# A two-layer encoder trunk: the whole output projection of layer 0 moves into the list schedule, in three rounds, with the residual kept in SBUF

## The chip, the cores and the metric

The kernel runs on one core of a Trainium2 chip. The metric is the device time of one execution in microseconds (us). The kernel before took 1623.58 us in the median of three runs (1622.95 to 1627.89).

## The reference

The input is one sequence of 512 tokens with 1024 channels. Layer 0 mixes with a bidirectional RWKV-7 half (8 heads of 64) and a bidirectional Hyena half (512 channels, long filters through an FFT); layer 1 mixes with 2-D neighbourhood attention. Behind each mixer stand a gated convolutional FFN (width 2816) and a gated per-layer embedding, each added to the residual. The part that the change touches is this one:

```python
z = rmsnorm(h, mix_norm[j]) @ mix_w_in[j]
y_a = rwkv7_bidir(z[..., :RWKV_COLS], ...)          # channels 0 to 511
y_b = hyena_bidir(z[..., RWKV_COLS:], ...)          # channels 512 to 1023
h = h + jnp.concatenate([y_a, y_b], axis=-1) @ mix_w_out[j]
h = h + conv_ffn(h, ...)
h = h + per_layer_embedding(h, p[i], ...)
```

All products of large matrices are computed in float32 to nearly full precision.

## The kernel before

Activations lie channel-major: eight tiles of 128 channels by 512 tokens. A product with a weight is made of three matmuls in the fp32r type: each operand is split into a high part (a copy that rounds, on ScalarE) and a low part (the difference, on VectorE or GpSimd), and high x high, high x low and low x high are added in PSUM. One such matmul streams 512 columns through a 128 x 128 weight tile.

**Two ways of ordering.** Everything behind layer 0's mixer is written in the order in which it runs, by `gemm`: it loads a block of weights into `wraw` (L627), splits it into `whi` (ACT, L613) and `wlo` (DVE, L605) and issues the matmuls into the PSUM tiles `g` (L599). Layer 0's mixer is different. There `nc` is replaced by a recorder, class `Plan`: every call becomes a step with a cost and with the steps it depends on, and `schedule()` then sets the order of all steps on all five engines by a list schedule. Among the steps that can start soonest on an engine (within `AHEAD`) it takes the one with the highest rank: the longest chain of costs behind the step plus 1000 times a number per group from the table `ORDER`. `write()` issues the steps in that order (L562, so nearly all instructions of the mixer carry this line), and each engine keeps it. `nc.gates` holds a group back until some other step is planned. Of the tiles' names, `w` is a tile of the pool of slabs (44 of 128 x 520 values), `wr` a loaded weight tile (3 buffers), `wp` a split part (12 buffers), `b` a PSUM bank (8), `x` and `uv` what a scan loads and updates.

**The groups of the mixer.** `start` loads the input x (eight tiles `w<-in_xT`) and the constants, splits x into `xh`, `xl` and computes the RMS norm: `norm0` squares each tile on ACT and sums over channels with 32 one-column matmuls against a vector of ones (`b<-con,w`). `low` and `z` are the input projection of the RWKV half, `prep` its decays and keys, `inverse` a triangular inverse per head pair (through the DRAM tensors `nd` and `xd`), `scan` the state update over 8 chunks of 64 tokens, `out` its norm and gate, which gives `ys[0]` to `ys[3]`. `hyena` is the input projection of the other half; `filters`, `fparts`, `kf`, `signals`, `ab` and `back` are its convolution by Fourier tables (`dft_f`, `dft_i`), which gives `ys[4]` to `ys[7]`. `emb` computes the p projections of both layers ahead of time and stores them in DRAM (`pj_d`). `early` (`out_early`) multiplies `ys[0]` to `ys[2]` with their rows of the output weight, adds the input x, which it loads a second time, and stores the sum in the DRAM tensors `h_d`.

**Behind the mixer** `outproj0` (L1589) loads `h_d` back into the eight residual tiles `h` and runs the other five of eight rows of the output projection (`LATE`, 4 to 7 and 3) as ordinary `gemm`s: 2 groups of 4 output tiles x 5 rows x 3 = 120 matmuls. The FFN follows. Its `norm` scales the eight tiles into `xh`, `xl`, squares them on ACT into `nsq` (2 buffers) and adds the squares on GpSimd into `nacc`; the sums over channels are needed only at the evictions.

## Time and profile before

| what | us |
|---|---|
| median of three runs | 1623.58 |
| the profiled execution | 1624.16 |
| its span (first to last instruction) | 1622.4 |
| busy TensorE (PE) in it | 1544.8 |
| busy VectorE (DVE) | 978.7 |
| busy ScalarE (ACT) | 719.5 |
| busy GpSimd (POOL) | 325.4 |

About 1.8 us of the profiled execution lie outside its span. PE, DVE, ACT and POOL are engines that work side by side; SP only issues DMAs, in order. A row of the timeline gives the start in us from the span's start, the duration, the engine, the line, the operation, the tiles (out<-in) and the count of merged instructions; in brackets stands the idle time of the engine before it and what ended it. Matmuls overlap, so a row of several tells the pace by its start and the next row's start. fp32 matmuls appear as two records each in the trace and as one in the order.

### The profile page before, as it was taken

Reading aid. Unit: us, or ns where it says so; the run is one execution under the profiler, and the core shown is the slowest. Engines: PE = TensorE matmul, PEld = TensorE weight load, DVE = VectorE, ACT = ScalarE, POOL = GpSimd, SP = SyncE. Lnnn points to the kernel's source line nnn. Section 1 sums busy time; section 2 is a strip of 40 time slices with the busy share of each in tenths; the row PEclk is TensorE's granted clock in tenths of the full one; section 3 lists DMA queues with packets and bytes.
Section 4 is the critical chain, followed back from the end, with each engine's and each line's share of the span. In section 5 each row is a group of like instructions: output and inputs, shape, how many; then the busy total and the mean of one; then the engine's idle time right before and its main releaser. Section 6 shows DMA issues by size and latency. Waiting matters only on the chain.

```text
span 1622.4 us, 24675 instructions
## 1 busy us (share of the span) xinstructions
PE 1544.8 (95%) x9576; PEld 1227.8 (76%) x9576; DVE 978.7 (60%) x1609; ACT 719.5 (44%) x1206; POOL 325.4 (20%) x286
## 2 busy tenths in 40 slices
PE   8999999996886999999999999999999999999998
PEld 6767777764565888888888878778778888888886
DVE  2587585865553766624774664565675665366654
ACT  4553635663432544413443563655554443144332
POOL 3574445533240300000001322011030000000020
PEclk9999999997987999999999999999999999999999
DMA  6366456677454233232324232323112322222421
GB/s 215 96 190 181 133 154 177 214 220 215 145 179 141 100 100 104 91 101 95 95 100 144 90 130 91 111 81 126 61 65 92 104 93 102 91 87 95 166 94 65
DMA packets 116310, 200.16 MB, mean 123 GB/s; under 512 B 27729, under 2 KB 57297, under 8 KB 116194
## 3 DMA queue, kind: packets, MB, share of 16 engines
q1 hardware_dynamic: 116194, 198.59, 38.3%
q8 instruction: 75, 1.23, 0.3%
q14 instruction: 41, 0.34, 0.1%
HBM read 166.04 MB, written 30.93 MB: 121 GB/s over the span
## 4 chain that ended last, share of the span: by engine, by line
PE 85%; DMA 4%; DVE 4%; ACT 2%; SPq 2%; POOL 1%; issue 1%; DVEq 0%; POOLq 0%; ACTq 0%
PE g L599 62%; PE b L562 19%; DVE w L562 3%; SPq L562 2%; PE m L599 1%; PE s L599 1%; DMA wr<-in_dft_f 1%; PE m L1835 1%; POOL w L562 1%; DMA wr<-in_dft_i 1%; ACT w L562 1%; ACT oh L613 0%; DMA pj_d<-w 0%; DMA wr<-in_mix_w_in 0%; DVE ol L605 0%
## 5 line engine op out<-in xcount | busy, mean ns | idle before, releaser
L605 DVE TENSOR_TENSOR wlo<-wraw,whi 128x1024 fp32r<-128x1024 f32 x186 | 235.5, 1268 | 325.8 <-ACT whi L613 321.0
L613 ACT CAST whi<-wraw 128x1024 fp32r<-128x1024 f32 x186 | 193.5, 1041 | 424.4 <-PE g L599 408.1
L599 PE MATMUL g<-xh,whi 128*128 128x512 f32 x872 | 342.0, 392 | 13.2 <-ACT whi L613 13.2
L599 PE MATMUL g<-xh,wlo 128*128 128x512 f32 x872 | 340.6, 391 | 0.0
L599 PE MATMUL g<-xl,whi 128*128 128x512 f32 x872 | 340.3, 390 | 0.0
L599 PEld LDWEIGHTS g<-xh,whi 128*128 128x128 f32 x872 | 164.4, 188 | 48.5 <-ACT whi L613 13.4
L599 PEld LDWEIGHTS g<-xh,wlo 128*128 128x128 f32 x872 | 164.2, 188 | 35.3 <-DVE wlo L605 0.8
L599 PEld LDWEIGHTS g<-xl,whi 128*128 128x128 f32 x872 | 164.3, 188 | 33.9
L605 POOL TENSOR_TENSOR nacc<-nsq 128x512 f32<-128x512 f32 x5 | 9.2, 1833 | 777.3 <-PE g L599 639.7
L562 PE MATMUL b<-xh,wp 128*128 128x512 f32 x416 | 142.2, 416 | 9.1 <-ACT wp L562 9.1
L599 PE MATMUL g<-hh,whi 128*128 128x512 f32 x352 | 137.2, 390 | 0.0
L599 PE MATMUL g<-hh,wlo 128*128 128x512 f32 x352 | 137.0, 389 | 0.0
L599 PE MATMUL g<-hl,whi 128*128 128x512 f32 x352 | 137.0, 389 | 0.0
L602 DVE SCALAR_TENSOR_TENSOR c<-u,prm,c 128x511 f32<-128x511 f32 x176 | 126.5, 747 | 6.4 <-ACT c L608 5.9
L562 PEld LDWEIGHTS b<-xh,wp 128*128 128x128 f32 x416 | 77.8, 192 | 32.6 <-ACT wp L562 10.5
L608 ACT ACTIVATE c<-u,prm 128x512 f32<-128x512 f32 x88 | 70.3, 816 | 70.8 <-DVE u L605 70.8
L562 POOL TENSOR_TENSOR wp<-wr,wp 128x512 fp32r<-128x512 f32 x60 | 80.1, 1350 | 64.9 <-ACT wp L562 30.2
L562 PE MATMUL b<-w 64*64 64x128 f32 (+5 forms) x1692 | 84.3, 253 | 7.3 <-POOL w L562 3.5
L562 POOL TENSOR_TENSOR w<-w 128x256 f32<-128x256 f32 (+2 forms) x72 | 76.6, 1083 | 68.0 <-ACT w L562 41.4
L562 PE MATMUL b<-xl,wp 128*128 128x512 f32 x208 | 85.2, 417 | 0.0
L562 PEld LDWEIGHTS b<-w 64*64 64x64 f32 (+4 forms) x1692 | 62.9, 136 | 26.5 <-issue 9.2
L605 DVE TENSOR_TENSOR u<-g,rstd 128x512 f32<-128x512 f32 x104 | 71.4, 687 | 16.5 <-PE g L599 15.6
(170 smaller groups left out, 2563.4 us busy)
## 6 DMA issues: line engine op xcount, KB each, us to landing
wraw<-in_up SPq DMA_DIRECT2D x88, 512.0 KB, 3.4
wraw<-in_down SPq DMA_DIRECT2D x44, 512.0 KB, 3.5
wr<-in_mix_w_in SPq DMA_DIRECT2D x52, 256.0 KB, 2.9
wraw<-in_na_w_qkv SPq DMA_DIRECT2D x24, 512.0 KB, 3.5
x<-ch_d SPq DMA_DIRECT2D x16, 640.0 KB, 7.2
ch_d<-w SPq DMA_DIRECT2D x64, 128.0 KB, 2.0
wraw<-in_gate SPq DMA_DIRECT2D x16, 512.0 KB, 3.5
tab<-in_rpb SPq DMA_DIRECT2D x8, 768.0 KB, 4.2
```

The lines of the kernel that those rows point to most:

```text
L562: getattr(e, method)(*args, **kw)
L599: return self.nc.tensor.matmul(out, lhsT, rhs, start=start, stop=stop, skip_group_check=not group)
L602: return self.nc.vector.scalar_tensor_tensor(out=out, in0=in0, scalar=scalar, in1=in1, op0=op0, op1=op1)
L605: return (eng or self.nc.vector).tensor_tensor(out=out, in0=in0, in1=in1, op=op)
L608: return self.nc.scalar.activation(out=out, in_=in_, func=func, **kw)
L613: self.nc.scalar.copy(h, src)
L1835: nc.tensor.transpose(pst[:, i], sc[:, i // 2, (i % 2) * P:(i % 2 + 1) * P], ident)
```

## The change

The output projection is now wholly part of the list schedule, in three rounds that add into the residual tiles `h`: `early` (`ys[0]` to `ys[2]`, plus x), `mid` (`ys[4]` to `ys[7]`) and `last` (`ys[3]`), each for two groups of four output tiles. `outproj0` and the DRAM tensors `h_d` are gone. The tiles `h` are allocated before the mixer; x is loaded into them, and until `early` they also serve as scratch for `wa_up`, the low-rank tiles, `rstd0` and the filters' spectra. The pool of slabs shrinks from 44 to 39 and the scan's `x` from 4 buffers to 3. The sum of squares is added up on VectorE, so that 4 one-column matmuls are left of 32. The planner's rules change too: a change of a matmul's shape costs 0.17 in its account, a shape is kept for 1.5 us where another step of it is ready, groups named in `loose` need not wait for their own first step, and the numbers of `ORDER` are new, with a table `MOVED` of exceptions.

```diff
-    HOP, OWN, AHEAD = 0.2, 0.1, 0.2
-    DRAG, SMALL = 0.0, 5
+    HOP, OWN, AHEAD = 0.2, 0.1, 0.15
+    DRAG, SMALL = 0.0, 3
+
+    SWITCH, RUN = 0.17, 1.5
...
-                t, s = max((x for x in c if x[0] <= m), key=lambda x: x[1].rank)
+                c = [x for x in c if x[0] <= m]
+                if e == "tensor" and run < self.RUN:
+                    c = [x for x in c if x[1].form == form] or c
+                t, s = max(c, key=lambda x: x[1].rank)
...
+            ph = self.pool(top, "ph", side="right")
+            self.h = [ph.tile([P, S], F32, name=f"h{k}") for k in range(KT)]
             self.mixer0()
...
-                self.outproj0()
...
-            self.rstd0 = pk.tile([P, S], F32, name="rstd0")
+            self.rstd0 = self.h[4]
...
-            self.sl = self.pool(st, "sl", bufs=self.SLABS, side="right")
             self.wr = self.pool(st, "wr", bufs=3, side="right")
             self.wp = self.pool(st, "wp", bufs=self.PARTS, side="right")
+            self.sl = self.pool(st, "sl", bufs=self.SLABS, side="right")
...
-    SLABS, PARTS = 44, 12
-
-    ORDER = dict(start=200, low=190, filters=77, scan=100, inverse=90, prep=80, z=79, out=60, hyena=50,
-                 fparts=56, kf=39, signals=62, ab=44, back=59, early=30, emb=10)
+    SLABS, PARTS = 39, 12
+
+    ORDER = dict(start=180, x=200, low=198.5, norm=120, filters=75, scan=100, inverse=84, prep=80, z=79, out=60,
+                 hyena=50, fparts=40, kf=67, signals=70, ab=58, back=46, early=30, emb=25, consts=86, mid=72,
+                 last=99)
...
-        xin = [self.slab() for _ in range(KT)]
+        xin = self.h
         for k in range(KT):
+            nc.group = "x", k
             nc.sync.dma_start(out=xin[k], in_=a["xT"][k])
...
+        late = [self.weights("mix_w_out_b", g) for g in range(2)]
+        for g in range(2):
+            nc.gates["mid", g] = self.ys[7][:1]
+            self.part(("mid", g), self.out_late, g, LATE[:4], sources=late[g][:4])
+        for g in range(2):
+            nc.gates["last", g] = [self.ys[LATE[4]][0], ("mid", g)]
+            self.part(("last", g), self.out_late, g, LATE[4:], sources=late[g][4:])
...
+            if acc is None:
+                acc = sq
+            else:
+                self.tt(acc, acc, sq, ALU.add)
+        ps = self.bank(4)
+        for t in range(4):
+            self.mm(ps[:, t:t + 1], acc[:, t * P:(t + 1) * P], self.cst("one"))
...
-            x = xs[q] = rb.tile([P, 2, 5, 2, 64], F32, name="x", bufs=4)
+            x = xs[q] = rb.tile([P, 2, 5, 2, 64], F32, name="x", bufs=3)
...
-            self.tt(xin[j], ps, xin[j], ALU.add)
-            self.put(self.h_d[g * 4 + j], xin[j])
+            self.tt(self.h[g * 4 + j], ps, xin[j], ALU.add)
+
+    def out_late(self, g, ks):
+
+        w = [self.item(len(ks) > 1) for _ in ks]
+        for j in range(4):
+            ps = self.bank()
+            c = slice(j * P, (j + 1) * P)
+            for i, k in enumerate(ks):
+                self.mm3(ps, w[i][0][:, c], w[i][1][:, c], *self.ys[k], i == 0, k == ks[-1])
+            t = self.h[g * 4 + j]
+            self.tt(t, ps, t, ALU.add)
```

**The first loads.** On SP, the first rows of the program; `wr<-in_mix_w_in` are the weight tiles of the input projection. Before:

```order
L724 DMA prm<-in_params 128x126
L562 DMA w<-in_xT 128x512
L562 DMA wr<-in_mix_w_in 128x512 x3
L562 DMA w<-in_feats 17x512
L562 DMA w<-in_xT 128x512 x3
L562 DMA con<-in_const 128x387
L562 DMA w<-in_xT 128x512 x4
L562 DMA prm<-in_params 128x394
L562 DMA w<-in_wa_up 128x512 x2
L562 DMA rcon<-in_rconst 128x1088
L562 DMA gup<-in_g_up 128x512
L562 DMA wr<-in_mix_w_in 128x512 x3
```

And now, behind the first parameters, three tiles of x (`h_73` to `h_75`) and two weight tiles:

```order
L582 DMA h_76<-in_xT 128x512
L582 DMA wr<-in_mix_w_in 128x512
L582 DMA h_77<-in_xT 128x512
L582 DMA h_78<-in_xT 128x512
L582 DMA h_79<-in_xT 128x512
L582 DMA h_80<-in_xT 128x512
L582 DMA con<-in_const 128x387
L582 DMA rcon<-in_rconst 128x1088
L582 DMA gup<-in_g_up 128x512
L582 DMA h_73<-in_wa_up 128x512
L582 DMA prm<-in_params 128x394
L582 DMA wr<-in_mix_w_in 128x512
```

All of x now stands ahead of every constant, and the fourth weight tile behind five loads of constants and parameters.

**The end of the mixer on TensorE.** Before, the inverse transform (`b<-w`, 96 matmuls of 256 columns) ran last, and the out-projection's 120 matmuls into `g` followed:

```order
L562 MATMUL b<-xl_672,w 128x512
L562 MATMUL b<-xh_671,w 128x512 x4
L562 MATMUL b<-w 128x256 x96
L599 MATMUL g<-xh_1150,whi 128x512
L599 MATMUL g<-xl_1151,whi 128x512
```

Now the inverse transform is followed by `early` of one group, the 96 matmuls of `mid`, the 24 of `last` (`xh_811`, `xl_812` are `ys[3]`) and the 48 of layer 1's `emb` (`b<-w,wp`), of which 38 stand in one row just ahead of these; the next `g` belongs to the FFN:

```order
L582 MATMUL b<-xh_811,wp 128x512 x3
L582 MATMUL b<-w,wp 128x512 x2
L582 MATMUL b<-xh_811,wp 128x512
L582 MATMUL b<-xl_812,wp 128x512
L582 MATMUL b<-xh_811,wp 128x512
L582 MATMUL b<-w,wp 128x512 x8
L619 MATMUL g<-xh_6042,whi 128x512
L619 MATMUL g<-xl_6043,whi 128x512
```

No product of the mixer stands behind the eight `emb` matmuls.

**The way into the FFN on ScalarE.** Before, the casts of the out-projection's weights came first and the FFN's scaled tiles and squares were mixed among them:

```order
L562 CAST xh_1162<-w 128x512
L613 CAST whi<-wraw 128x1024 x2
L613 CAST whi<-wraw 128x512
L613 CAST whi<-wraw 128x1024 x2
L608 ACTIVATE xh_6067<-h_5873,prm 128x512
L608 ACTIVATE nsq<-h_5873 128x512
L613 CAST whi<-wraw 128x512
L608 ACTIVATE xh_6071<-h_5874,prm 128x512
```

Now (`COPY w<-b` evicts `emb`'s products, which SP then stores in `pj_d` ahead of the FFN's first weight load):

```order
L582 COPY w<-b 128x512 x4
L628 ACTIVATE xh_6062<-h_78,prm 128x512
L628 ACTIVATE xh_6066<-h_79,prm 128x512
L628 ACTIVATE xh_6070<-h_80,prm 128x512
L628 ACTIVATE nsq<-h_73 128x512
L628 ACTIVATE nsq<-h_74 128x512
L628 ACTIVATE nsq<-h_75 128x512
L628 ACTIVATE nsq<-h_76 128x512
L628 ACTIVATE nsq<-h_77 128x512
L633 CAST whi<-wraw 128x1024
```

The FFN's first weight cast now stands behind three scaled tiles and five squares, with no matmuls of the mixer left beside it.

More of the change, by code (lines that the diff above doesn't have):

```diff
@@ L291, in note @@
             first = self.firsts.setdefault(self.group, s)
-            if first is not s:
+            if first is not s and self.group not in self.loose:
                 s.after[first.n] = True
@@ L339, in price @@
                 t = max(n / 600, 0.223)
+            form = tuple(32 if x <= 32 else 64 if x <= 64 else P for x in (rows, cols))
+            if s.form is None:
+                s.form = form
+            elif form != s.last:
+                t += self.SWITCH
+            s.last = form
             s.cost += t
@@ L447, in start @@
             return t
[L449 removed]
+        lifted, form, run = False, None, 0.0
         while True:
@@ L480, in schedule @@
                     c *= 2
+                if s.form != form:
+                    run = 0.0
+                    c += self.SWITCH
+                form, run = s.last, (run if s.form == s.last else 0.0) + s.cost
             if s.table and s.table != table:
@@ L484, in schedule @@
                 taken[e].append((t, t + c))
-            free[e] = end = t + c
+            s.issue, free[e] = t, t + c
+            end = t + c
             if s.bytes:
@@ L511, in schedule @@
                 x.left -= 1
-                x.at = max(x.at, end + (self.HOP if x.engine != e or s.bytes else self.OWN))
+                x.at = max(x.at, end + (self.HOP if x.engine != e or s.bytes else 0.0 if e == "tensor" else self.OWN))
                 if not x.left:
```

77 lines of the change are left out of this document (37 added, 40 removed).

## The prediction

> **What bounds the kernel now.** I first read the page's shares and slices, then the busy time of each engine by stage, cut where the program changes its work, and then the chain of waits and the timeline at the places where TensorE (PE) stands still.
>
> ```profile
> PE 1544.8 (95%) x9576; PEld 1227.8 (76%) x9576; DVE 978.7 (60%) x1609; ACT 719.5 (44%) x1206; POOL 325.4 (20%) x286
> 0.00:24.40 24.40, 17.04 (x70) 15.27 (x71) 7.29 (x13) 13.96 (x23) 5.86 (x19) 1.00 0.89 300
> 24.40:362.50 338.10, 329.11 (x3395) 244.25 (x3395) 234.67 (x440) 179.69 (x378) 177.84 (x170) 0.98 0.56 166
> 362.50:495.10 132.60, 101.18 (x976) 75.19 (x976) 72.42 (x135) 47.01 (x110) 46.81 (x41) 0.85 0.56 174
> 495.10:508.30 13.20, 0.04 (x1) 0.04 (x1) 4.83 (x9) 2.26 (x3) 0.00 (x0) 0.70 0.65 217
> 508.30:538.60 30.30, 30.26 (x121) 24.31 (x122) 16.68 (x17) 11.74 (x17) 4.82 (x3) 0.91 0.35 114
> 538.60:1622.40 1083.80, 1067.21 (x5017) 868.71 (x5015) 642.83 (x999) 464.86 (x679) 90.06 (x53) 0.99 0.30 99
> ```
>
> Columns of a stage: its length, then busy time of PE, weight loads, DVE, ACT and POOL, the granted clock, the DMA share and GB/s. PE bounds the program, 95% busy, so time can come only from its idle stretches, its slow clock, or its work. The last row, the FFN and all behind it, is 1083.8 us that the change does not touch. The change acts on the 538.6 us ahead: the start, the dense middle (97% busy), the end of the mixer (PE idle for 132.6 - 101.18 = 31.4 us, clock 0.85), a hole of 13.2 us, and the out-projection's 120 matmuls in 30.3 us.
>
> ```profile
> 381.52 2.93 PE L562 MATMUL b<-w,wp 128*128 128x512 f32 x6 [13.53 <-ACT wp L562]
> 412.98 1.22 PE L562 MATMUL b<-w,wp 128*128 128x512 f32 x2 [4.99 <-ACT wp L562]
> 501.35 5.79 DMA wraw<-in_mix_w_out_b
> 508.26 0.79 PE L599 MATMUL g<-xh,whi 128*128 128x512 f32 x1 [13.18 <-ACT whi L613]
> ```
>
> Two timeline rows, one of the chain, one more of the timeline: 18.5 of the 31.4 us are two waits for Fourier tables, and the hole is the wait for the out-projection's first weight, whose load could start only when the mixer's tiles were free.
>
> **The start (term A).**
>
> ```profile
> 5.25 0.72 ACT L562 ACTIVATE xh<-w,prm 128x512 fp32r<-128x512 f32 x1
> prm<-in_params SPq DMA_DIRECT2D x1, 63.0 KB, 1.9
> 6.00 0.75 DVE L562 SCALAR_TENSOR_TENSOR xl<-w,prm,xh 128x512 fp32r<-128x512 f32 x1 [2.88 <-ACT xh L562]
> 10.76 13.81 PE L562 MATMUL b<-con,w 128*128 128x1 f32 x64 [0.31 <-DMA con<-in_const]
> 18.27 0.62 ACT L562 CAST wp<-wr 128x512 fp32r<-128x512 f32 x1 [1.36 <-DMA wr<-in_mix_w_in]
> 0.00:24.40 24.40, 3.40 (x6) 1.66 (x7) 3.49 (x6) 5.01 (x4) 1.00 0.89 300
> ```
>
> The row of `prm` is from the page's list of DMA issues, with its time from issue to landing. The last row is the first stage cut to instructions on `wp` (PE, weight loads, ACT, POOL): by 24.4 us PE had run six matmuls of the input projection and 64 records of the norm, which held it from 10.76 on while the squares arrived one by one. Now only 8 such records remain, later. Ahead of the eighth tile of x stand 63 KB of parameters, 7 more tiles and 3 weight tiles, 2.88 MB with itself; at the window's 300 GB/s that is 9.6 us, and with 1.9 us for the first landing and 0.72 + 0.75 for the split, all of x is ready near 13.5 us and PE has done its 36 first matmuls at 14.5. The fourth weight tile lies 1.70 MB further on, 5.7 us: with landing and cast (0.62) near 18.5 us. From there to 24.4 PE runs 25 more at the 0.235 us found below: 61 instead of 6, 55 x 0.235 = 12.9 us, less 0.9 for the 8 records still to come. **A = 12 us.** Bounds: 7 if the five constant loads delay the fourth weight by 5 us more than their bytes; 16 if loads never hold PE back after 14.5. The seven additions of squares on DVE (7 x 0.61) run beside PE.
>
> **Fewer changes of shape (term B).**
>
> ```profile
> 346.54 0.70 PE L562 MATMUL b<-w,wp 128*128 128x512 f32 x2
> 347.17 0.45 PE L562 MATMUL b<-x,uv 128*64 128x64 f32 x8
> 348.17 1.64 PE L562 MATMUL b<-w,wp 128*128 128x512 f32 x6
> 349.74 0.45 PE L562 MATMUL b<-x,uv 64*64 64x64 f32 x8
> ```
>
> From its start to that of the next row, a run of two takes 0.63 us and one of six 1.57: each matmul 0.235, and 0.16 for the change to another shape. Counted over PE's rows of the two orders, the mixer changes shape 275 times before and 220 now. 55 x 0.16 = 8.8 is the upper bound; where PE waits anyway it is worth nothing. **B = 5 us**, since most changes lie in the dense middle.
>
> **The end of the mixer (term C).** The 120 out-projection matmuls cost the same inside the list, 120 x 0.235 = 28.2 us, and so stay in the sum. What can be gained is the 31.4 us of idle time and the slow clock: at most 0.15 x 101 = 15 us of busy time lost, of which I count 9, because the mean of 0.85 contains the idle stretches. That is 40 us. For cover there are now `emb`'s 96 matmuls (22.6 us), which the order moves from the middle to this stage, and `mid` behind the inverse transform. What is late next, from the order's distances and these rows:
>
> ```profile
> w<-kt_d SPq DMA_DIRECT2D x16, 128.0 KB, 7.0
> w<-in_xT SPq DMA_DIRECT2D x16, 256.0 KB, 4.6
> wr<-in_dft_i SPq DMA_DIRECT2D x8, 256.0 KB, 5.2
> 133.77 2.72 DMA xd<-w
> 145.41 64.74 PE b L562 x839
> L562 DVE TENSOR_TENSOR w<-w 128x512 f32<-128x512 f32 (+16 forms) x120 | 70.5, 609 | 9.8 <-DMA w<-nd 7.2 <-DMA w<-hw_d 0.6
> L562 POOL TENSOR_TENSOR w<-w 128x512 fp32r<-128x512 f32 x16 | 20.6, 1301 | 19.9 <-ACT w L562 19.8
> ```
>
> The last inverse's round trip through `xd` took 133.77 to 145.41 = 11.6 us in head pair 0; the order leaves some 8 us of matmuls beside it: 4 us of wait. Scan 3 needs the `kt_d` loads, 7.0 us, with ten matmuls (2.3) beside them: 5. The spectra put 26 additions and products on DVE (26 x 0.61 = 16 us) and 13 on POOL (17 us) beside the last scan, whose own DVE steps queue behind them, with 21 us of PE work there: 4. `dft_i` is loaded behind four other tiles, 5.2 us and a cast, with 4 us of matmuls left: 3. The second `early` has its weights behind four reloads of x (4.6 us): 3. Together 19 us, and 4 for the clock behind them: 23 stay, **C = 40 - 23 = 17 us**; bounds 0 and 40.
>
> **The way into the FFN (term D).**
>
> ```profile
> 509.50:513.90 4.40, 4.38 (x10) 3.47 (x11) 1.83 (x2) 0.52 (x1) 0.00 (x0) 0.50 0.70 235
> 528.52 1.16 ACT L608 ACTIVATE nsq<-h 128x512 f32<-128x512 f32 x2 [1.08 <-POOL nacc L605]
> L562 ACT COPY w<-b 128x512 f32<-128x512 f32 (+2 forms) x96 | 43.8, 477 | 41.5 <-PE b L562 40.8
> L608 ACT ACTIVATE xh<-h,prm 128x512 fp32r<-128x512 f32 x40 | 32.2, 818 | 13.8 <-DVE h L605 13.8
> L608 ACT ACTIVATE nsq<-h 128x512 f32<-128x512 f32 x40 | 28.2, 721 | 6.0 <-POOL nacc L605 5.7 <-DVE h L605 0.2
> L605 POOL TENSOR_TENSOR nacc<-nacc,nsq 128x512 f32<-128x512 f32 x30 | 49.8, 1659 | 74.4 <-ACT nsq L608 73.1
> L613 ACT CAST whi<-wraw 128x1024 fp32r<-128x1024 f32 x186 | 193.5, 1041 | 424.4 <-PE g L599 408.1 <-DMA wraw<-in_mix_w_out_b 8.2 <-issue 7.8
> wraw<-in_up SPq DMA_DIRECT2D x88, 512.0 KB, 3.4
> ```
>
> The hole does not go; it moves behind the last `emb` matmul. From there ACT has about two of four copies left (1.0), three scaled tiles (2.5), two squares (1.4); then the squares wait for POOL, as they did at 528.52, because `nsq` has two buffers: an addition (1.7), a square (0.7), an addition (1.7), a square (0.7), and only then the cast (1.0): 10.7, say 11 us. The first weight, issued behind the last store of `pj_d` (four copies 1.9, and the issues), would land after 2.5 + 3.4 and be cast at 7; that bounds it from below, and 5.1 us, as this load's sibling needed, does not exceed 11. So 13.2 becomes 11 and both are followed by the same half clock (ten matmuls in 4.4 us where 19 fit, 2.1 us lost): **D = 2 us**; bounds 5 (a hole of 8) and -2.
> The page "TensorE: Matmul & The Clock Gate" of the Trainium skill, section "Architectural detail: the array is 16× 32×32, not 1× 128×128", says that ScalarE and VectorE take their instructions strictly first in, first out. By this rule the cast must wait behind the squares and D stays at 2; if a ready cast could overtake them, D would be 5 and the sum 3 us more. The 1.08 us of ACT idle time at 528.52, with other work queued behind, agree with the rule.
>
> **At no cost.** The `h_d` stores and loads (16 of 256 KB) go; their time is inside the hole. `h` as scratch and 5 slabs fewer free about as much as they take. With 3 buffers a load of the scan's `x` starts once the pair of chunks three places earlier is done, so two pairs of chunks cover it; what it costs without that cover is the last rival.
>
> **Sum.** A 12 + B 5 + C 17 + D 2 = 36 us. The profiled execution took 1624.2 us (1622.4 and 1.8 around it), 0.6 above the median of the runs: 1624.2 - 36 = 1588 us, and 1588 to the nearest microsecond against the median too.
>
> **The rivals.**
>
> *Nearly every wait at the end is covered* (20%). `emb`, `mid` and `last` are 216 matmuls, 51 us of work that needs little else, and a list schedule puts them where PE has nothing else. Then only 5 of the 40 us stay: 12 + 5 + 35 + 2 = 54, 1570 us. Against it: in the order most of `mid` stands behind the last inverse transform, so it cannot cover what lies ahead.
>
> *The end keeps its waits; the three rounds do not do what they say* (18%). `mid` depends on `ys[4]` to `ys[7]`, which come last; if loads through SP's one queue and the in-order DVE and POOL set the pace, the same 31.4 us stay, in other places. C = 0: 12 + 5 + 2 = 19, 1605 us.
>
> *No change that can be measured* (4%): A and B are eaten by the middle, which loses `emb` as cover (24.4 to 362.5 has only 9 us of idle time now) and gains 30.
>
> *Slower: the scan runs out of `x`* (8%).
>
> ```profile
> x<-ch_d SPq DMA_DIRECT2D x16, 640.0 KB, 7.2
> 361.41 0.40 PE L562 MATMUL b<-uv,w 128*64 128x64 f32 x8
> 365.24 0.45 PE L562 MATMUL b<-uv,w 128*64 128x64 f32 x8 [0.52 <-ACT uv L562]
> ```
>
> Two loads of each of the four scans can no longer run ahead into the scan before. If SP holds each until its buffer is free and issues it with nothing in between, 8 x 7.2 = 58 us are exposed: 1588 + 58 = 1646 us. It decides from the point where a load is issued less than 7.2 us ahead of its chunk. Against it: a chunk took 365.24 - 361.41 = 3.8 us with PE nearly free, and two pairs of chunks, 15 us, lie between.
>
> **How the numbers follow.** My forecast has 50%. About 0.3%, 5 us, can be told from no change. The forecast and the first two rivals, 88%, are faster; 4% the same; 8% slower. The bounds of the terms give 7 + 0 + 0 - 2 = 5 us and 16 + 9 + 40 + 5 = 70 us, 1619 and 1554. For 8 of 10 I take 1560 to 1612 us, which holds the first two rivals and leaves the far ends out.
>
> **What would show it.** A: the norm's 64 records shrunk to 8, and PE dense from 18 to 20 us on. B: fewer, longer runs of one shape in the timeline. C: the two waits of 13.5 and 5 us gone, PE idle for about 20 us in the last third of the mixer, and waits for `kt_d`, `dft_i` and DVE in place of `dft_f`. D: a hole of some 11 us ahead of the first `g`, ended by ACT's `whi`, with squares that wait for POOL just before. The forecast is wrong if the middle falls below 97% busy, if the hole is closed, or if scan matmuls wait for `x`.

## The result

The changed kernel takes 1599.7 us in the median of four runs (1595.4 to 1603.9), the kernel before 1625.7 in the same job: ratio 0.984, 95% interval 0.981 to 0.987. A second measurement of the changed kernel gave 1600.8 us and 0.983 (0.981 to 0.985). It is faster, by 26 us between the medians and 25.0 between the spans of the two profiled executions (1622.4 and 1597.4), where 36 were forecast, and lies inside the range of 1560 to 1612. Two runs far above all others, 1923.4 us of the kernel before and 5203.6 us of the version with the new norm alone, are left out of medians and ratios.

The page of the profile after, its span and the shares of the engines:

```profile
span 1597.4 us, 24570 instructions
PE 1527.6 (96%) x9520; PEld 1217.7 (76%) x9520; DVE 975.3 (61%) x1618; ACT 718.5 (45%) x1210; POOL 341.6 (21%) x296
```

The stages of the kernel before, cut at 300 us (columns as in the prediction: length, busy time of PE, weight loads, DVE, ACT, POOL, granted clock, DMA share, GB/s):

```profile
24.40:300.00 275.60, 269.47 (x2545) 200.03 (x2546) 188.53 (x355) 137.15 (x280) 151.20 (x144) 0.99 0.51 149
300.00:495.10 195.10, 160.81 (x1827) 119.40 (x1826) 118.55 (x220) 89.55 (x206) 73.45 (x68) 0.88 0.63 196
```

And of the kernel after: start, middle, end of the mixer, hole, first matmuls of the FFN, the rest:

```profile
0.00:24.40 24.40, 15.49 (x58) 11.77 (x59) 15.60 (x20) 14.60 (x24) 10.26 (x22) 1.00 0.89 292
24.40:300.00 275.60, 265.45 (x2856) 198.66 (x2854) 197.02 (x390) 146.00 (x306) 143.97 (x144) 0.97 0.56 159
300.00:499.40 199.40, 175.15 (x1593) 135.87 (x1592) 121.05 (x213) 87.99 (x196) 92.34 (x76) 0.91 0.55 173
499.40:508.30 8.90, 0.05 (x1) 0.05 (x1) 2.60 (x5) 6.62 (x12) 4.07 (x4) 0.69 0.82 295
508.30:516.60 8.30, 7.33 (x17) 5.30 (x18) 5.43 (x3) 3.56 (x5) 7.42 (x4) 0.51 0.53 147
516.60:1597.40 1080.80, 1064.14 (x5001) 866.04 (x4999) 633.59 (x990) 459.70 (x670) 83.52 (x49) 0.99 0.30 99
```

The mixer of before ended at 495.1 us and left 28.2 us of out-projection to do; now everything is done at 499.4. The middle became worse, 10.2 us of idle time in place of 6.1 and a clock of 0.97 in place of 0.99; the end of the mixer became better, 24.3 us of idle time (199.40 - 175.15) in place of 34.3 (195.10 - 160.81). The hole is 8.9 us in place of 13.2, but 17 matmuls behind it take 8.3 us at a clock of 0.51, 4.0 at their full pace.

**One table for all versions.** The order differs between versions, so a window does not hold the same work. I therefore counted: each matmul of an order at its pace at full clock (0.229 us for 512 columns of fp32r, the others from stretches of the trace in which PE ran dense), summed in the order and laid over the trace. *Lag* is the time minus the work issued by then. The 28 extra one-column matmuls of the old norm, 6.2 us, and 12.3 us of added ones in one experiment count as lag, since they produce nothing.

| version | lag at 50 us | at 300 us | at the mixer's end | its growth from 300 us on |
|---|---|---|---|---|
| before | 25.1 | 39.3 | 94.6 | 55.3 |
| after | 11.0 | 29.0 | 71.4 | 42.4 |
| after, second measurement | 9.8 | 33.3 | 75.9 | 42.6 |
| norm's 32 matmuls back, ahead | 23.5 | 28.9 | 83.8 | 54.9 |
| before, with the new norm alone | 16.0 | 46.6 | 94.3 | 47.7 |
| delay in the same order | 32.8 | 48.9 | 90.5 | 41.6 |
| old numbers | 10.5 | 28.2 | 81.3 | 53.1 |
| emb early again | 11.0 | 30.4 | 93.5 | 63.1 |
| last two rounds outside | 10.5 | 30.6 | 72.9 | 42.3 |
| no keeping, no price of shape | 10.7 | 47.2 | 113.9 | 66.7 |
| price of shape, no keeping | 10.6 | 53.6 | 113.7 | 60.1 |
| squares added on DVE | 10.8 | 30.6 | 74.9 | 44.3 |
| last stores on POOL | 10.3 | 24.7 | 68.2 | 43.5 |
| both: rounds outside, stores on POOL | 10.1 | 26.5 | 66.9 | 40.4 |

Between before and after the lag falls by 14.1 us at the start, rises by 3.8 in the middle (14.2 to 18.0), falls by 12.9 at the end: 23.2. The hole gives 4.3 more. From the FFN's first matmul to the end the kernel takes 1597.4 - 508.25 = 1089.15 us, 5.35 more than the 1083.8 behind the old out-projection; the old half clock had cost 2.1, so 3.3 are lost there. Together 24.2 of the 25.0 us; the rest is the paces in the count. (In the second profile of the changed kernel the middle loses 9.3 in place of 3.8, and the clock behind the hole 0.3 in place of 3.3.)

### The profile page after: what moved, and what is told of

It reads as the page before. It is cut to its first block, busy times and chain, and to the rows that moved or that the text cites. A ratio compares the mean times of both kernels' runs of the same rounds, so it can differ in the third digit from the quotient of the medians.

```text
span 1597.4 us, 24570 instructions
## 1 busy us (share of the span) xinstructions
PE 1527.6 (96%) x9520; PEld 1217.7 (76%) x9520; DVE 975.3 (61%) x1618; ACT 718.5 (45%) x1210; POOL 341.6 (21%) x296
## 4 chain that ended last, share of the span: by engine, by line
PE 82%; DVE 6%; DMA 4%; ACT 3%; SPq 2%; issue 1%; POOL 1%; POOLq 0%; DVEq 0%; ACTq 0%
PE g L619 61%; PE b L582 17%; DVE w L582 4%; SPq L582 2%; PE m L619 2%; PE s L619 1%; DMA wr<-in_mix_w_in 1%; PE m L1878 1%; POOL w L582 1%; ACT w L582 1%; DMA w<-nd 1%; DMA wr<-in_dft_f 1%; POOL nacc L625 0%; ACT oh L633 0%; DVE uv L582 0%
## 5 line engine op out<-in xcount | busy, mean ns | idle before, releaser
L625 DVE TENSOR_TENSOR wlo<-wraw,whi 128x1024 fp32r<-128x1024 f32 x180 | 227.8, 1267 | 322.5 <-ACT whi L633 317.7
L619 PE MATMUL g<-xh,whi 128*128 128x512 f32 x832 | 326.8, 393 | 8.9 <-ACT whi L633 8.9
L619 PE MATMUL g<-xh,wlo 128*128 128x512 f32 x832 | 325.3, 391 | 1.0 <-DVE wlo L625 1.0
L619 PE MATMUL g<-xl,whi 128*128 128x512 f32 x832 | 325.0, 391 | 0.0
L619 PEld LDWEIGHTS g<-xh,whi 128*128 128x128 f32 x832 | 157.0, 189 | 43.1 <-ACT whi L633 9.3
L619 PEld LDWEIGHTS g<-xh,wlo 128*128 128x128 f32 x832 | 156.8, 189 | 34.7 <-DVE wlo L625 1.7
L619 PEld LDWEIGHTS g<-xl,whi 128*128 128x128 f32 x832 | 157.1, 189 | 32.4
L582 PE MATMUL b<-xh,wp 128*128 128x512 f32 x432 | 149.9, 420 | 10.3 <-ACT wp L582 10.0
L582 DVE TENSOR_TENSOR w<-w 128x512 f32<-128x512 f32 (+16 forms) x116 | 69.1, 613 | 17.6 <-DMA w<-nd 10.7
L619 PE MATMUL g<-wlo,xh 128*128 128x512 f32 x192 | 77.2, 402 | 0.0
```

What stands on the lines that cost most here:

```text
L582: getattr(e, method)(*args, **kw)
L619: return self.nc.tensor.matmul(out, lhsT, rhs, start=start, stop=stop, skip_group_check=not group)
L625: return (eng or self.nc.vector).tensor_tensor(out=out, in0=in0, in1=in1, op=op)
```

## The experiments

Ratios are to the kernel before, in the same job; a median is compared with 1599.7 and 1600.8 us of the changed kernel.

### The norm's matmuls back at the front

```diff
-                self.tt(acc, acc, sq, ALU.add)
-        ps = self.bank(4)
-        for t in range(4):
-            self.mm(ps[:, t:t + 1], acc[:, t * P:(t + 1) * P], self.cst("one"))
+                pass
+            for t in range(4):
+                self.mm(ps[:, t:t + 1], sq[:, t * P:(t + 1) * P], self.cst("one"), k == t == 0, k == KT - 1 and t == 3,
+                        group=False)
...
-    ORDER = dict(start=180, x=200, low=198.5, norm=120, filters=75, scan=100, inverse=84, prep=80, z=79, out=60,
+    ORDER = dict(start=180, x=200, low=198.5, norm=201, filters=75, scan=100, inverse=84, prep=80, z=79, out=60,
```

> The changed kernel, with one part of the start undone: the sum of squares is again made of 32 one-column matmuls, placed by the planner ahead of the input projection as before; the order of the first loads stays. My theory is that the norm's records, and not the loads, were what held TensorE: then the records stand between the first input-projection matmuls again while the squares arrive one by one, z of head pair 0 ends at about 53 us in place of 40.5, and the time is 1599.7 + 12 = 1612 us. The rival, that the order of the loads gave the gain, has TensorE wait for weights and not for squares: only the 28 matmuls themselves come back, at 0.22 us each 6 us, z of head pair 0 ends at about 46, and the time is about 1606 us.

Measured: 1610.2 us, ratio 0.990 (0.987 to 0.994), and z of head pair 0 ends at about 52 us. Both are near what the theory of the records said. But the table tells another story: the 12.5 us of lag at 50 us are gone at 300 (28.9 against 29.0), and the loss comes in the end stage (54.9 against 42.4). The planner made another order there, so this run does not say what time at the start is worth. The table is of the fastest of its four runs (1603.7 us); there the hole ahead of the FFN is 5.2 us in place of 8.9, which gives back a part of the 12.4 us that the lag at the mixer's end has grown by.

### The new norm alone, in the kernel before

```diff
+            if acc is None:
+                acc = sq
+            else:
+                self.tt(acc, acc, sq, ALU.add)
+        nc.group = "norm"
+        ps = self.bank(4)
+        for t in range(4):
+            self.mm(ps[:, t:t + 1], acc[:, t * P:(t + 1) * P], self.cst("one"))
...
-    ORDER = dict(start=200, low=190, filters=77, scan=100, inverse=90, prep=80, z=79, out=60, hyena=50,
+    ORDER = dict(norm=120, start=200, low=190, filters=77, scan=100, inverse=90, prep=80, z=79, out=60, hyena=50,
```

> The kernel before with one part of the change: squares added on VectorE, four one-column matmuls behind them in place of 32, placed by the planner behind the first input-projection matmuls; the first loads, tiles and numbers stay. If the norm's records alone held the start, z of head pair 0 ends 12 us earlier than 53.9 us, and the kernel before becomes 8 to 13 us faster: 1613 to 1619 on the scale of 1627. If the order of the first loads is needed as well, TensorE waits for x and weights instead and the gain is 6 us or less.

Measured: 1625.8 us, ratio 1.000 (0.998 to 1.002). Neither theory: the lag at 50 us falls by 9.1 us, and the middle gives back more than that (46.6 against 39.3 at 300 us). At the mixer's end the lag is that of the kernel before (94.3 and 94.6), and the hole behind it is 16.5 us in place of 13.2. This order is another one too, with 288 changes of shape in place of 275. In the middle PE now runs at a lower clock; of this version, to be read against 0.98 and 1.00 of the kernel before in the same stretches:

```profile
50.00:150.00 100.00, 93.24 (x841) 68.84 (x839) 71.11 (x144) 52.61 (x97) 60.65 (x67) 0.90 0.57 164
150.00:300.00 150.00, 146.22 (x1850) 105.82 (x1848) 104.30 (x219) 76.48 (x180) 70.55 (x66) 0.95 0.58 163
```

### A delay at the start, in an unchanged order

```diff
+            n = 15 if s.group == "norm" and s.engine == "tensor" and self.width(s.calls[0][1][0]) == 1 else 1
-            for method, args, kw in s.calls:
+            for method, args, kw in s.calls * n:
```

> The changed kernel in exactly its own order, but the four one-column matmuls of the first norm are issued 15 times in place of once (the same values each time), near 27 us. At 0.22 us each the 56 added matmuls delay everything behind them on TensorE by 12 us, the size of the prediction's term A, without moving anything. If time won at the start is time won at the end, the kernel is 12 us slower, 1613 us. If the middle of the mixer is set by work on other engines that TensorE waits for a little later (the kernel before with the new norm alone gained nothing), the delay is taken up there: z of head pair 0 ends 12 us later, the stretch from 50 to 300 us has a higher clock and fewer waits, and the time is 1600 to 1606 us.

Measured: 1622.0 us in 12 runs (1615.9 to 1633.8), ratio 0.998 (0.996 to 1.000), 21 us more than the changed kernel. The delay was larger than meant, 22.4 us where z of head pair 0 ends (62.9 against 40.5). In the profiled run 15 to 19 us of it are left at the mixer's end, and the medians differ by 21. So in this order two thirds or more of the time at the start is time at the end, and term A counts for the most part. Why 56 matmuls cost 22 us stands in the windows of this run:

```profile
26.79 20.84 PE L583 MATMUL b<-con,w 128*128 128x1 f32 x120
27.00:30.50 3.50, 3.50 (x34) 3.50 (x33) 0.00 (x0) 1.25 (x3) 1.26 (x1) 1.00 0.41 129
34.00:37.50 3.50, 3.50 (x18) 3.50 (x18) 0.00 (x0) 0.00 (x0) 0.00 (x0) 0.50 0.00 0
48.00:51.50 3.50, 3.50 (x10) 2.66 (x9) 0.00 (x0) 1.14 (x2) 3.50 (x4) 0.50 0.07 23
51.50:55.00 3.50, 3.50 (x17) 2.86 (x16) 1.03 (x2) 0.89 (x2) 1.17 (x1) 0.86 0.58 200
```

The first row is one of the timeline, the others are windows. The records begin at 34 in 3.5 us; a few us later the granted clock is 0.50, though PE is busy for 3.50 of 3.50 us, and they go at 18 in 3.5 us, 0.19 us each. The matmuls behind them start at half clock too.

### The old numbers

```diff
-    ORDER = dict(start=180, x=200, low=198.5, norm=120, filters=75, scan=100, inverse=84, prep=80, z=79, out=60,
-                 hyena=50, fparts=40, kf=67, signals=70, ab=58, back=46, early=30, emb=25, consts=86, mid=72,
-                 last=99)
+    ORDER = dict(start=180, x=200, low=198.5, norm=120, filters=77, scan=100, inverse=90, prep=80, z=79, out=60,
+                 hyena=50, fparts=56, kf=39, signals=62, ab=44, back=59, early=30, emb=10, consts=86, mid=29,
+                 last=28)
...
+    MOVED = {}
```

> The changed kernel with the group numbers of the kernel before for all groups that it had (scan, inverse, filters, kf, signals, ab, back, early, emb), without the table of exceptions, and with mid and last just below early. If the three rounds and the residual in SBUF are what shortened the end of the mixer, the time stays within 5 us of 1599.7. If the new numbers are, then the waits for Fourier tables and for the last inverse come back ahead of the rounds, some 13 to 17 us of idle time in the last third of the mixer, and the time is 1613 to 1617 us.

Measured: 1611.6 us, ratio 0.9905 (0.988 to 0.993); the growth from 300 us on is 53.1 us, almost that of the kernel before. The new numbers are worth 11 to 12 us. In the two profiles the difference is 13.9 us: 9.9 at the mixer's end, all of it from 300 us on, and 4.0 in the hole and behind it. The waits there, by what ended them (us in total, times, longest), of the changed kernel:

```profile
PE b L582 <- ACT uv L582: 11.0, 10, 2.9
PE b L582 <- DVE uv L582: 4.5, 5, 1.6
PE b L582 <- ACT wp L582: 1.8, 1, 1.8
```

And with the old numbers:

```profile
PE b L582 <- ACT uv L582: 10.1, 10, 2.6
PE b L582 <- ACT wp L582: 6.7, 2, 4.0
PE b L582 <- DVE w L582: 4.5, 3, 2.1
PE b L582 <- ACT w L582: 3.9, 3, 2.2
```

The kernel before, with the same columns:

```profile
PE b L562 <- ACT wp L562: 18.5, 2, 13.5
PE b L562 <- ACT uv L562: 3.0, 5, 1.0
PE b L562 <- DVE uv L562: 1.9, 2, 1.2
```

The waits for split weights and Fourier tables (`wp`), 18.5 us in the kernel before, are 1.8 with the new numbers and 6.7 with the old. The second theory is near in size (12 us where 13 to 17 were expected), though less than half of those waits came back: the remainder of the loss is in waits for DVE and ACT, in the clock, and behind the mixer. There the order puts the whole sum of squares of the FFN's norm ahead of the first weight cast, and the first `g` starts 16.9 us behind the mixer's last matmul, at 526.25, in place of 8.9:

```profile
521.37 1.87 PE L619 MATMUL m<-con,nacc 128*128 128x1 f32 x8 [12.06 <-POOL nacc L625]
```

Which other part of the change spares the old numbers the 13.5 us wait was not tried.

### The second and third round outside

```diff
-            self.part(("mid", g), self.out_late, g, LATE[:4], sources=late[g][:4])
...
-            self.part(("last", g), self.out_late, g, LATE[4:], sources=late[g][4:])
...
+                    self.gemm("mix_w_out_b", g, 0, len(LATE), lambda k: self.ys[LATE[k]], evac)
                 self.ffn(0)
```

> The changed kernel without the second and third round in the list schedule: the 120 matmuls on ys[3] to ys[7] run behind the mixer as ordinary gemms again, into the residual tiles in SBUF; start, numbers, tiles and early stay. If mid and last cover waits in the mixer, those waits come back: the mixer's part on TensorE is longer than 499.4 - 28.2 = 471.2 us by 10 us or more, the hole is 13 us as before, and the time is about 1612 us. The rival: the rounds run behind the last wait of the mixer and cover nothing in it, so the mixer ends near 471 to 475 us, and only the hole differs (13.2 in place of 8.9): 1600 to 1606 us.

Measured: 1597.0 us, ratio 0.981 (0.979 to 0.984). The rival holds. Up to the last matmul of `early` for group 0 the order on PE is the same, and that matmul ends at 461.5 us here, at 459.3 and 463.5 in two profiles of the changed kernel. So `mid` and `last` cover nothing: they stand behind the last long wait (one of 0.7 us follows in the changed kernel). The hole in front of the gemms is 6.5 us, and it is now ended by the load alone, which SP issued behind the last store. Timeline of this version, PE, SP and ACT:

```profile
480.00 0.79 PE L619 MATMUL g<-xh,whi 128*128 128x512 f32 x1 [6.53 <-ACT whi L633]
467.31 7.21 SPq L582 DMA_DIRECT2D pj_d<-w  x8
478.90 1.04 ACT L633 CAST whi<-wraw 128x1024 fp32r<-128x1024 f32 x1 [4.74 <-DMA wraw<-in_mix_w_out_b]
```

### emb early again

```diff
-                 hyena=50, fparts=40, kf=67, signals=70, ab=58, back=46, early=30, emb=25, consts=86, mid=72,
+                 hyena=50, fparts=40, kf=67, signals=70, ab=58, back=46, early=30, emb=62, consts=86, mid=72,
```

> The changed kernel with emb's number raised from 25 to 62, so that its 96 matmuls run in the middle again, as in the kernel before, and are not left for the end. By the prediction's term C they cover 22.6 us of waits in the last third: without them the idle time from 300 to 500 us grows by 10 to 20 us and the time is 1610 to 1620 us. If emb mostly runs behind the last wait, as its second half does now, it covers little: the time stays within 5 us of 1600.8, and the hole ahead of the FFN changes its neighbours only.

Measured: 1618.1 us, ratio 0.9955 (0.993 to 0.998), 17 us more, as term C expected. `emb` now runs from 309 to 357 us, and behind the last scan PE stands still twice, once behind DVE. PE and DVE of this version:

```profile
450.91 2.07 PE L582 MATMUL b<-w,con 128*128 128x512 f32 x2 [10.57 <-DVE w L582]
462.84 1.12 PE L582 MATMUL b<-con,w 128*128 128x128 f32 x4 [6.48 <-ACT w L582]
441.14 4.90 DVE L582 TENSOR_TENSOR w<-w 128x512 f32<-128x512 f32 x8
446.56 4.30 DVE L582 TENSOR_TENSOR w<-w 128x512 f32<-128x512 f32 x7
```

The hole ahead of the FFN is 5.2 us here, 3.6 less than in the changed kernel, so the mixer itself lost more than the 17 us (22.1 of lag at its end). With `emb` in the middle the Fourier groups come later, and in the order on DVE the products and sums of both spectra (`ab`) stand ahead of the first step of the last `out`: the two rows hold 15 such steps of 0.61 us, with which that `out` waits. In the changed kernel they lie among the chunks of scan 3 and are done before it ends, and `emb`'s first half, from 348 to 402 us, fills PE in the meantime.

### The planner without its rules on shape

```diff
-    SWITCH, RUN = 0.17, 1.5
+    SWITCH, RUN = 0.0, 0.0
```

> The changed kernel with a planner that prices a change of the matmul's shape at nothing and keeps no shape (0.17 and 1.5 us both set to 0). The prediction's term B: the mixer changes shape some 55 times more and the time is 5 us more, 1605 us, in the dense middle above all. The rival: longer runs of one shape put the small matmuls together, and stretches of them are followed by a low clock; then the middle gets its clock of 0.99 back and the time is the same or up to 5 us less, 1595 to 1600 us.

Measured: 1631.7 us, ratio 1.002 (1.0005 to 1.003): 31 us more, and neither theory comes near. The second run leaves the price and takes the keeping away:

```diff
-    SWITCH, RUN = 0.17, 1.5
+    SWITCH, RUN = 0.17, 0.0
```

> The changed kernel with a planner that still prices a change of shape at 0.17 but keeps no shape (1.5 us set to 0): 264 changes of shape in place of 220, 275 in the run with both at 0. If the keeping is what was worth 31 us there, the time is again 1620 to 1632 us. If the planner only has to know the price to place the rest well, the time is 1600 to 1608 us. By the prediction's count the 44 changes cost 44 x 0.16 = 7 us at most.

Measured: 1634.0 us, ratio 1.004 (1.003 to 1.006). It is the keeping that matters. The 55 and 44 changes of shape themselves, at 0.16 us, are 9 and 7 us; the rest is waits and clock. Between its first matmul and the mixer's end PE is idle for 56 us in both, 36 in the changed kernel, and the clock falls early. First this stretch of the changed kernel, then of the version without both rules:

```profile
50.00:150.00 100.00, 95.44 (x838) 70.94 (x839) 72.56 (x141) 49.99 (x95) 54.77 (x56) 0.94 0.58 166
```

```profile
50.00:150.00 100.00, 89.37 (x750) 62.83 (x749) 72.71 (x140) 50.01 (x89) 53.41 (x60) 0.85 0.54 153
```

What these runs leave open: how much belongs to keeping a shape, and how much to numbers that fit only the planner they stand with. Each of the four versions with another plan and the rest of the change (these two, the old numbers, `emb` early) is 11 to 34 us slower, more together than the whole change gained, so these prices cannot be added. Nor were the smaller parts of the change undone one by one: `AHEAD` and `SMALL`, the price of the planner's DVE steps, the groups in `loose`, the sizes of the pools and the residual in SBUF.

### The hole: squares added on VectorE

```diff
-                self.tt(new, acc, sq, ALU.add, nc.gpsimd)
+                self.tt(new, acc, sq, ALU.add, nc.gpsimd if self.planned else nc.vector)
```

> The changed kernel with the additions of squares of the FFN's first norm on VectorE (0.6 us each) in place of GpSimd (1.3 us); the order on ScalarE stays: five squares, then the first cast. If the squares' pace on GpSimd sets the hole, as the prediction's term D says, the cast starts once the load has landed, near 506 in place of 507.2, the hole shrinks from 8.9 to 7.5 us or less and the time by 1.5 to 2.5 us. If the weight load sets it, the hole and the time stay within 0.5 us; a median cannot tell 2 us here, the trace's hole can.

The hole of the changed kernel, PE and ACT:

```profile
508.25 0.79 PE L619 MATMUL g<-xh,whi 128*128 128x512 f32 x1 [8.87 <-ACT whi L633]
504.63 1.15 ACT L628 ACTIVATE nsq<-h 128x512 f32<-128x512 f32 x2 [1.43 <-POOL nacc L625]
506.63 0.63 ACT L628 ACTIVATE nsq<-h 128x512 f32<-128x512 f32 x1 [0.85 <-POOL nacc L625]
507.17 1.03 ACT L633 CAST whi<-wraw 128x1024 fp32r<-128x1024 f32 x1
```

And of this version:

```profile
510.56 0.79 PE L620 MATMUL g<-xh,whi 128*128 128x512 f32 x1 [7.68 <-ACT whi L634]
```

Measured: 1596.4 us, ratio 0.982 (0.978 to 0.985), not told apart from the changed kernel. The hole is 1.2 us shorter, so the squares' pace on POOL was what ended it, by about what was expected. The cast came 5.15 us behind the issue of its load here and 6.37 in the changed kernel, so in the changed kernel the load had most likely landed before the squares let the cast go.

### The last stores on GpSimd

```diff
-        self.put(self.pj_d[l * 8 + g * 4 + j], t)
+        (nc.gpsimd if l else nc.sync).dma_start(out=self.pj_d[l * 8 + g * 4 + j], in_=t)
```

> The changed kernel with one edit: the eight stores of the last p projection are issued by GpSimd's queue in place of SP's, so that the FFN's first weight load is not queued behind them. If the load's place in SP's queue and the squares ahead of the cast make the hole of 8.9 us, the load lands before TensorE has finished the mixer, the first cast stands behind two squares in place of five, the hole is 4 to 6 us, the slow clock behind it is shorter, and the time is 3 to 6 us less: 1594 to 1597 us. If the squares' pace on GpSimd alone sets it, the eight issues on GpSimd, ahead of the additions, leave the hole at 9 us or make it longer, and the time stays at 1600 us.

Measured: 1595.3 us (1588.7 to 1598.4), ratio 0.980 (0.9775 to 0.982). That is 4 to 6 us less than the changed kernel, as expected, though the intervals of the ratios overlap. The hole is 4.8 us, and the first cast stands behind two squares:

```profile
501.10 0.79 PE L619 MATMUL g<-xh,whi 128*128 128x512 f32 x1 [4.82 <-ACT whi L633]
```

With the rounds outside as well:

> The changed kernel without the second and third round in the list schedule (120 matmuls as gemms behind the mixer again) and with the eight stores of the last p projection on GpSimd's queue. In the run without the rounds the hole of 6.5 us was ended by the first weight load, issued on SP behind the last store and landing 4.3 us later. If that queue is the cause, the load now lands before TensorE has finished the mixer, the hole shrinks to 1 to 3 us, less time at half clock follows, and the time is 5 to 8 us below the run without the rounds: 1589 to 1592 us. If the hole is set by the time when the mixer's tiles are free, it stays at 6.5 us and the time at 1597.

Measured: 1591.5 us, ratio 0.978 (0.976 to 0.980), 9 us less than the changed kernel in the same job. This version beats both kernels. The time is the one expected, the reason is not: its hole is 5.8 us, hardly less than 6.5: the load was issued at 467.55, as soon as PE had done its last matmul of the mixer at 467.47, so it waited for a tile and no longer for the queue. PE and SP of this version:

```profile
473.29 0.80 PE L619 MATMUL g<-xh,whi 128*128 128x512 f32 x1 [5.83 <-ACT whi L633]
467.55 11.23 SPq L647 DMA_DIRECT2D wraw<-in_mix_w_out_b  x6
```

The other 6 us against the version with the rounds outside alone arose inside the mixer, whose order is the same in both; the next run bears on that.

### The changed kernel again

No edit.

> The changed kernel itself, so that the versions derived from it have a measurement with as many runs beside them. Its four runs spread over 8.5 us. If the spread is chance of the clock (short waits in the middle that are followed by half clock in one execution and not in another), the median is again about 1.6% below the kernel before, with single runs from 1592 to 1604 us, and the profiled execution shows other stretches of low clock in the middle than the first one. If the first runs were an accident, the ratio moves by over 0.3%.

Measured: 1600.8 us (1600.3 to 1601.4), ratio 0.983 (0.981 to 0.985). The order of the mixer up to `early` of group 0 is identical in six profiled versions: twice the changed kernel, rounds outside, squares on DVE, and the two with stores on POOL. It ends there at 459.3, 463.5, 461.5, 462.9, 456.1 and 455.6 us. The paths part between 150 and 300 us, first at one wait in the first scan; in the changed kernel's second profile, and then in the version with the stores on POOL:

```profile
185.67 0.45 PE L582 MATMUL b<-uv,w 128*64 128x64 f32 x6 [2.43 <-DVE uv L582]
```

```profile
183.33 0.45 PE L582 MATMUL b<-uv,w 128*64 128x64 f32 x6 [1.23 <-DVE uv L582]
```

The wait is 2.4 us in the four versions without stores on POOL, 1.2 and nothing in the other two, and by 200 us these two lie 2.7 to 4.5 us ahead of the four. In those two nothing that was edited runs ahead of that matmul. Whether the stores act in some way or it is chance, two profiles cannot say; so of the 9 us that the best version gains over the changed kernel, only the 3.0 of the hole (8.9 to 5.8) are explained.

## Why the prediction was right and wrong

**A, the start, 12 us: right in size, wrong in its reason.** Measured 13.4 us at z of head pair 0 (53.9 to 40.5) and 14.1 in lag. The prediction said that the 64 records held PE "while the squares arrived one by one". PE did not wait for squares: the records went at half pace. 64 took 13.81 us, 0.22 each, one every 0.21 us from the first to the last, though the last square was done at 16.91 us; in the changed kernel 8 go at twice that pace, as their row and the next one of its timeline show:

```profile
26.41 0.95 PE L582 MATMUL b<-con,w 128*128 128x1 f32 x8
27.22 0.48 PE L582 MATMUL b<-xl,wp 128*128 128x512 f32 x1
```

That is 0.81 us for 8, 0.10 each. The run with 120 of them shows both paces and the clock between them; that the clock was also the cause in the kernel before is concluded from the pace. Rows of the kernel before, ACT's last square and PE ahead of the records and behind them:

```profile
16.30 0.61 ACT L562 ACTIVATE w<-w 128x512 f32<-128x512 f32 x1
8.68 0.63 PE L562 MATMUL b<-xl,wp 128*128 128x512 f32 x1
9.11 1.34 PE L562 MATMUL b<-xh,wp 128*128 128x512 f32 x2
25.00 1.91 PE L562 MATMUL b<-xh,wp 128*128 128x512 f32 x4
26.71 1.05 PE L562 MATMUL b<-xl,wp 128*128 128x512 f32 x2
```

From 8.68 to 9.11 one matmul took 0.43 us, and from 25.00 to 26.71 four took 0.43 each, in place of 0.235. So here the records did not lower the clock: they found PE at half pace and left it there until 29.3 us. The clock column of the profile reads 1.00 at this place; the pace, not the column, tells of the half clock. The order of the first loads, which the prediction worked through in detail, was the changed kernel's in the run with the records back (up to the small constants), and z ended late all the same.

The sum of A leaves out the half clock on both sides. The first eight matmuls of the changed kernel go at half pace too, and 58 had run by 24.4 us where 61 were counted, 0.7 us less than forecast. The 11 behind the records in the kernel before took 24.43 to 29.27, 0.44 each, 2.3 us more than at full pace. With both, 12 becomes 13.6, near the 13.4 measured. Two slips are small: the 8 records are set at 0.9 us, half of what the prediction's own row gives (8 x 0.22 = 1.7), and took 0.81; and the 2.88 MB ahead of the last tile of x leave out the 63 KB of parameters.

**B, changes of shape, 5 us in the middle: no gain there.** The middle from 24.4 to 300 us is 96.3% busy (265.45 of 275.60; 97.8% before), below the 97% that the prediction named as its own refutation, and has lost 4 us of lag (9 in the second profile). Over the prediction's own stretch, to 362.5 us, it is 93.0%, where the kernel before had 97.3%; from 300 us on this stretch holds the tail of scan 2, of which C speaks. The row of the changed kernel:

```profile
24.40:362.50 338.10, 314.45 (x3422) 236.52 (x3422) 244.05 (x490) 177.53 (x380) 178.05 (x172) 0.94 0.58 168
```

The changes of shape are 55 fewer, as counted; what that saved cannot be told from the larger loss beside it. The step that failed is pricing the rule by 55 x 0.16 alone, with no term in the sum for what the new order loses in the middle; the prediction named that loss only in the rival of no change, at 4%. In its place the runs show the plan as a whole: keeping a shape decides which step runs next, and with it when DVE and ACT get their input; without it the kernel loses over 30 us. The prediction's fear that the middle eats a gain was right in kind: PE's idle time there rose from 6.1 to 10.2 us and its clock fell from 0.99 to 0.97.

**C, the end of the mixer, 17 us: 12.9 measured, from another source.** Both table waits went, and about 24 us of idle time stayed from 300 us on, of 34 before, where some 20 were named for a shorter stretch. The waits left are not those listed: the last inverse, `kt_d` and `dft_i` cost almost nothing, while the scans' own steps (`uv`, through ACT and DVE) rose from 4.9 to 15.5 us, in the tails of scans 2 and 3, where the order has nothing else for PE. Rows of the changed kernel's timeline at the end of scan 2, the two longest of these waits and what DVE and ACT stood for just before:

```profile
337.01 0.45 PE L582 MATMUL b<-uv,w 128*64 128x64 f32 x8 [2.95 <-ACT uv L582]
345.27 1.02 PE L582 MATMUL b<-x,uv 128*64 128x64 f32 x8 [2.56 <-ACT uv L582]
334.42 0.69 DVE L582 TENSOR_TENSOR w<-w 128x512 f32<-128x512 f32 x1 [2.62 <-DMA w<-hw_d]
344.43 0.62 ACT L582 CAST w<-wr 128x512 fp32r<-128x512 f32 x1 [2.46 <-DMA wr<-in_pT]
```

The scan's `uv` steps on DVE (336.37) and ACT (344.95) come behind these two in their engine's order. So in both places the scan stood behind a step of another group whose load had not landed; the second rival named such a cause, for DVE and POOL.

The cover is `emb`, as the step said (17 us slower with it in the middle), and the new numbers (11 to 12 us without them; `emb`'s is one of them, so the two overlap), but not `mid`: the 120 matmuls of the rounds in the schedule cover nothing. The rival that the rounds do not do what they say is true of the rounds and false of the time.

**D, the hole, 2 us: 1.0 measured, 4.0 in the second profile.** 8.9 us in place of the forecast 11, since the additions on POOL ahead of the cast took 1.26 us each and not 1.7, and the scaled tiles and squares on ACT a little less than counted; and it was ended as foretold, by the cast behind squares that wait for POOL. What was mis-sized is the slow clock: the prediction let it cost 2.1 us as before. With a 0.97 us wait for `wlo` the stretch behind the hole was 5.35 us longer here (15 matmuls until full pace, which lose 4.4 of it), and 2.4 in the second profile, where full pace was back after 9; the hole was 8.9 us in both. The strict order on ScalarE, for which the prediction named the Trainium skill, is what the run with squares on DVE agrees with: the cast went ahead by 1.2 us when the squares ahead of it did.

**The rivals.** No wait for the scan's `x` is among PE's waits, so three buffers do. Nearly every late wait covered (1570) would have needed `mid` ahead of the waits, against which the prediction argued rightly. The forecast's sum missed by 11 us: 9 in the middle (B and the loss there), 4 in C and 1 in D, less 2 that A gave more, and 1 that the count leaves.

## What to carry to other kernels

When a list schedule is changed by its numbers, its rules and its work at once, the parts cannot be priced one by one: an edit that keeps the order measures a cost, one that lets the planner order anew measures another plan. Before counting work that is moved into a schedule as cover, see on which side of the last wait it stands. And count matmuls by what they do for the clock too: many tiny ones can slow what comes behind them.

## What the runs showed of the hardware

A TensorE that is busy without a gap can lose its clock: with one-column matmuls alone, PE busy for 3.50 of 3.50 us, the granted clock went from 1.00 to 0.50, and came back only when large matmuls had run for about 5 us (0.86 in 51.5 to 55.0). The run with the norm's records back shows the same: its first 19 records start 0.11 us apart, the others 0.21. Nor did such records bring a low clock back: in the kernel before, 13.81 us of them left PE at half pace. The page "TensorE: Matmul & The Clock Gate" of the Trainium skill, section "What's actually happening", names an idle window as what leads to the half rate and sustained busy time as what releases it; by that, if the profile's busy time is the measure, these records should have kept the full clock, and here they did not.

The same order of instructions does not give the same time: the same matmul ended between 455.6 and 463.5 us, with one wait of 2.4 us in some profiles and none in another.
